# Moving the sample states' turns and updates out of the group scans and beside the feed-forward layers, with new pools for the merge

## The chip, the cores and the metric

The kernel runs on one core of a Trainium2 chip. Five engines work side by side, each in its own order: TensorE (PE; PEld is its loading of weights), VectorE (DVE), ScalarE (ACT), GpSimd (POOL) and SyncE (SP), which here only issues transfers. An instruction starts when what stands before it on its engine is done and the semaphores that it waits for have come. The metric is the time of one execution in microseconds (us), as the median of several runs. A profiled execution gives the trace from which the rows below are read.

## The reference

One layer of a hybrid decoder is applied to 512 prompt rows and to 64 sample rows (8 sequences of 8 new positions), all in fp32:

```
h  = x + 0.5 * SwiGLU_1(rms(x))
u  = rms(h) @ W_in   -> z | xBC | dt | q | k | v | f | g_ssd | g_att
y_ssd = SSD(z, conv(xBC), dt)      (4 groups of 8 heads, state 64 x 128 per head, chunks of 128)
y_att = attention(q, k, v, f)      (the samples also see 2048 cached rows each)
h  = h + W_out(sigmoid(g_ssd) * (y_ssd @ W_ssd) + sigmoid(g_att) * (y_att @ W_att))
y  = h + 0.5 * SwiGLU_2(rms(h))
```

The part that matters here is the recurrent state of the samples. Each of the 8 sequences brings a state h0 of 32 heads x 64 x 128, and its 8 rows are one short chunk of the scan:

```
y_off[t]  = exp(acs[t]) * (C[t] . h0)              the old state seen by the new rows
h_new     = exp(acs[last]) * h0 + sum_s w[s] * x[s] (outer) B[s]     the new state, an output
```

## The kernel before

The 576 rows stand as columns: an activation tile has 128 features on its partitions and 576 columns, worked in two halves of 288. Every fp32 product is made of three products of fp32r operands: value = hi + lo, and hi·hi, hi·lo and lo·hi are summed in one PSUM bank (`mm3`, lines 208 to 210). For a weight block, loaded by SP in "stage" tiles of 512 KB (four buffers), `split` makes hi on ACT (`whi`, line 173) and lo on DVE or POOL (`wlo`, line 174), four buffers each. For an activation, `hilo` does it with an ACT copy (line 217) and a DVE subtraction (line 218).

The stages follow each other: the first feed-forward layer (to about 560 us, with the start of the input projection, 22 hidden blocks in two parts of 12 and 10, each followed by 8 output blocks), input projection and attention (to about 1010 us), the scans of the four groups (1010 to 1400 us), the last group's output and the merge of the two branches, the product with W_out (to about 1460 us), and the second feed-forward layer (to the end).

In a group's scan stand the convolution of the next group (`group_in`, `xr` at line 1046), the chunks of the prompt (`chunk`, with the decay tiles `dk`, line 1216, and the diagonal product, line 1241), the state carried from chunk to chunk, the gate (`gate`, with `zt` loaded from DRAM into one buffer), and eight of the 32 sample states. A state tile is 128 x (4 x 128), 256 KB: four sequences of one pair of heads. `state` loads it (`h0`), turns it with four TensorE transposes (line 1273), copies the turned tile with ACT (`hT`, line 1275), multiplies it with C (`cz`, line 1277), multiplies the unturned tile with its decay on POOL (`decp`, line 1278), makes the update with one matmul (line 1280), adds it on DVE (line 1281) and stores the tile. The operands of the update matmul are built in the function `updates` from 96-partition tiles that SP and ACT gather. Three buffers of the tag `h0` serve the states and these gathered tiles.

The merge follows group_out of the last group. For each of eight column tiles j it loads `th` (SP) and `mt` (ACT) from DRAM, computes (th + 1)·accs on DVE (line 1358), adds mt on POOL (line 1359, the last tile on DVE), and splits the sum into `xh` and `xl`. The product with W_out needs all eight split tiles for each of its eight column blocks; `hts`, loaded from hD at line 1369, is added at line 1380.

The code is written in the order of the stages, but a scheduler of the framework decides each engine's order from a timeline that it simulates itself; `soon()` raises the priority of what stands in it. Buffers of a pool are given out again when the last reader of the former tile is done, and an instruction that writes into one waits for that.

## Time and profile before

| | before |
|---|---|
| median of 3 runs | 1915.45 us (1914.47 to 1915.89) |
| profiled execution | 1914.71 us |
| its span, first to last instruction | 1912.9 us |
| granted TensorE clock, mean | 0.988 of full speed |
| TensorE busy | 1840.0 us, 96% |
| DVE, ACT, POOL busy | 1065.6, 748.2, 652.2 us |
| moved by DMA | 243.21 MB, 127 GB/s in the mean |

Busy times are sums over the whole span, so they say which engine is nearest to its limit but not where; the views by stretch do that. In a row of groups, "x32 | 39.8, 1244 | 3.7 <-PE tr L1273 3.7" means 32 instructions, 39.8 us together, 1244 ns in the mean, and 3.7 us in which the engine stood still ahead of them, ended by TensorE's tr at line 1273. ACTq, SPq and DVEq are the engines' queues: issues of transfers and waits for semaphores, which are not counted as busy. A clock of 1.00 is full speed, 2.4 GHz; 0.50 is the lower level, 1.2 GHz.

### The profile page before, as it was taken

The numbers are of one execution on the slowest core, as the hardware profiler recorded it, in microseconds if no ns is written. First come the engines' busy times: TensorE is split into PE (matmuls) and PEld (weight loads), VectorE is DVE, ScalarE is ACT, GpSimd is POOL, SyncE is SP. The second block draws the span as 40 slices with busy tenths as digits, with TensorE's granted clock in tenths as the row PEclk, the third lists the DMA queues.
The fourth block names the chain that finished last, engine by engine and source line by source line (L and its number), as shares of the span: only waits on it lengthen the run. The fifth ranks groups of instructions, "written<-read, shape, count | busy, mean of one in ns | idle before, by whom it ended". The sixth has DMA issues, their size and how long they took to land. (4 is left out here: it accounts for less than half of the span.)

```text
span 1912.9 us, 38609 instructions
## 1 busy us (share of the span) xinstructions
PE 1840.0 (96%) x15335; PEld 1731.7 (91%) x15335; DVE 1065.6 (56%) x2204; ACT 748.2 (39%) x1553; POOL 652.2 (34%) x719
## 2 busy tenths in 40 slices
PE   7999999999998999999998988989999999999999
PEld 7999999999896888888997877878889999999998
DVE  4554334445234777775729767888785544334432
ACT  4233223334222555554427455555434333223322
POOL 0433012322322344432227455675744233003310
PEclk9999999999998999999999999999999999999999
DMA  5432223234534787865465545464654332222322
GB/s 152 112 96 80 89 78 89 83 105 111 145 109 129 188 255 223 246 200 148 95 174 153 141 127 142 111 178 124 174 155 136 89 88 77 80 74 81 88 90 71
DMA packets 270841, 243.21 MB, mean 127 GB/s; under 512 B 53276, under 2 KB 243404, under 8 KB 270508
## 3 DMA queue, kind: packets, MB, share of 16 engines
q1 hardware_dynamic: 208208, 169.35, 32.4%
q10 hardware_dynamic: 53092, 36.79, 6.4%
q0 software_dynamic: 9360, 34.61, 5.6%
q8 instruction: 121, 1.98, 0.4%
q14 instruction: 60, 0.49, 0.1%
HBM read 204.97 MB, written 29.03 MB: 122 GB/s over the span
## 5 line engine op out<-in xcount | busy, mean ns | idle before, releaser
L173 ACT ACTIVATE whi<-stage 128x512 fp32r<-128x512 f32 (+2 forms) x474 | 294.6, 622 | 732.4 <-PE acc L209 640.6
L208 PE MATMUL acc<-xh,whi 128*128 128x288 f32 x1856 | 561.7, 303 | 17.8 <-DVE xr L1046 11.5
L209 PE MATMUL acc<-xl,whi 128*128 128x288 f32 x1856 | 552.6, 298 | 0.0
L210 PE MATMUL acc<-xh,wlo 128*128 128x288 f32 x1856 | 552.3, 298 | 0.0
L174 DVE TENSOR_TENSOR wlo<-stage,whi 128x512 fp32r<-128x512 f32 (+1 forms) x373 | 271.9, 729 | 263.9 <-ACT whi L173 243.8
L208 PEld LDWEIGHTS acc<-xh,whi 128*128 128x128 f32 x1856 | 351.0, 189 | 24.8 <-DVE xr L1046 11.5
L209 PEld LDWEIGHTS acc<-xl,whi 128*128 128x128 f32 x1856 | 351.3, 189 | 2.1 <-issue 1.5
L210 PEld LDWEIGHTS acc<-xh,wlo 128*128 128x128 f32 x1856 | 350.7, 189 | 2.0 <-issue 1.3
L338 POOL TENSOR_TENSOR u<-u,s 128x288 f32<-128x288 f32 x88 | 92.1, 1048 | 484.3 <-DVE u L337 427.7
L208 PE MATMUL pv<-xh,whi 128*128 128x288 f32 (+1 forms) x784 | 231.4, 296 | 2.4 <-ACT xh L220 2.2
L209 PE MATMUL pv<-xl,whi 128*128 128x288 f32 (+1 forms) x784 | 231.9, 296 | 0.6 <-DVE xl L218 0.6
L210 PE MATMUL pv<-xh,wlo 128*128 128x288 f32 (+1 forms) x784 | 231.6, 296 | 0.0
L174 POOL TENSOR_TENSOR wlo<-stage,whi 128x512 fp32r<-128x512 f32 (+1 forms) x101 | 138.2, 1368 | 269.6 <-ACT whi L173 255.6
L208 PEld LDWEIGHTS pv<-xh,whi 128*128 128x128 f32 (+1 forms) x784 | 147.3, 188 | 2.9 <-ACT xh L220 2.4
L209 PEld LDWEIGHTS pv<-xl,whi 128*128 128x128 f32 (+1 forms) x784 | 147.2, 188 | 1.2 <-DVE xl L218 0.8
L210 PEld LDWEIGHTS pv<-xh,wlo 128*128 128x128 f32 (+1 forms) x784 | 147.2, 188 | 0.2
L340 POOL TENSOR_TENSOR hl<-u,hh 128x288 fp32r<-128x288 f32 x88 | 77.5, 882 | 81.6 <-ACT hh L339 81.6
L208 PE MATMUL pv<-hh,whi 128*128 128x288 f32 x352 | 104.4, 296 | 0.0
L209 PE MATMUL pv<-hl,whi 128*128 128x288 f32 x352 | 104.3, 296 | 0.0
L208 PE MATMUL acc<-hh,whi 128*128 128x288 f32 x352 | 104.1, 296 | 0.0
L210 PE MATMUL acc<-hh,wlo 128*128 128x288 f32 x352 | 104.1, 296 | 0.0
L209 PE MATMUL acc<-hl,whi 128*128 128x288 f32 x352 | 104.1, 296 | 0.0
(335 smaller groups left out, 3470.0 us busy)
## 6 DMA issues: line engine op xcount, KB each, us to landing
stage<-in_w_in_dram SPq DMA_DIRECT2D x52, 512.0 KB
stage<-in_ffn_w_up_dram SPq DMA_DIRECT2D x44, 512.0 KB
stage<-in_ffn_w_gate_dram SPq DMA_DIRECT2D x43, 512.0 KB
stage<-in_ffn_w_down_dram SPq DMA_DIRECT2D x40, 512.0 KB
pb<-pastD SPq DMA_DIRECT2D x32, 256.0 KB
ab<-cumD SPq DMA_DIRECT2D x32, 256.0 KB
h<-in_state_ssm_dram SPq DMA_DIRECT2D x32, 256.0 KB
out_dram<-h ACTq DMA_DIRECT2D x32, 256.0 KB
```

Of the source, the lines that this page charges most:

```text
L173: act(hi, view, AF.Copy)
L174: e.tensor_tensor(lo, view, hi.bitcast(F32), ALU.subtract)
L208: mm(out, lhsT=hi, rhs=a, start=first and i == 0, stop=False)
L209: mm(out, lhsT=hi, rhs=b, start=False, stop=False)
L210: mm(out, lhsT=lo, rhs=a, start=False, stop=last and i == n - 1)
L338: G.tensor_tensor(u, u, sil[half], ALU.mult)
L340: G.tensor_tensor(hl[:, hs(half)], u, hh[:, hs(half)].bitcast(F32), ALU.subtract)
```

## The change

A state is taken apart into three pieces. Its turning (`turns`) is done beside the first feed-forward layer: from the fifth hidden block on, behind each block, one state is loaded, transposed, copied by ACT and stored turned to DRAM (`hTD`). Its product with C stays in the scan, where `state` now loads the turned tile into one of four buffers. Its update (`updates`) is done beside the second feed-forward layer, one state behind each block: the scan only stores the update's operands to DRAM (`operands`, into `upxD` and `upbD`); there they are loaded, the state is loaded a second time, and the decay product and the addition are one fused DVE operation for each of four pieces of 128 x 128, with the matmul's PSUM bank as its second operand. `decp` moves to the pool that lives for the whole kernel. `zt` has two buffers in place of one.

The merge is written into two new pools: `mg`, with three buffers each for `th` and `mt`, and `mhl`, with eight each for the split tiles `mh` and `ml`. Before, it took its tiles from the scan's pools, and its split tiles from the pool that held the mixer's operands; that place is now taken by the operands of the last norm. In the scan's pool, small tiles that shared the tags `h0` and `hT` now share a tag `x4`.

```diff
...
+    def place(h, t):
+        return (4 * h * 32 + 2 * t) * 64 * P, [(P, P), (32 * 64 * P, 4), (1, P)]
...
+    def turns(wait):
+        for _ in range(wait):
+            yield
+        with pool("turn", side="right", reuse_waits="tile") as sp_:
+            for t in range(16):
+                for h in range(2):
+                    h0 = tl(sp_, [P, 4, P], tag="h0", bufs=4)
+                    nc.sync.dma_start(out=h0, in_=ap3(A["state_ssm"][0], *place(h, t)))
+                    ps = tr()
+                    for b in range(4):
+                        nc.tensor.transpose(ps[:, b * P:(b + 1) * P], h0[:, b, :], ident)
+                    hT = tl(sp_, [P, 512], tag="hT", bufs=3)
+                    act(hT, ps, AF.Copy)
+                    nc.scalar.dma_start(out=hTD[h, t], in_=hT)
+                    yield
...
+    def updates():
+        with pool("upd", side="right", reuse_waits="tile") as sp_:
+            for g in range(4):
+                for h in range(2):
+                    r = slice(32 * h, 32 * (h + 1))
+                    xu = tl(sp_, [96, 512], F32R, tag="xu", bufs=2)
+                    bu = tl(sp_, [96, P], tag="bu", bufs=2)
+                    for k, (u, v) in enumerate(((0, 0), (0, 1), (1, 0))):
+                        nc.sync.dma_start(out=xu[32 * k:32 * (k + 1)].bitcast(F32), in_=upxD[g, u, r])
+                        nc.sync.dma_start(out=bu[32 * k:32 * (k + 1)], in_=upbD[g, v, r])
+                    bs = tl(sp_, [96, 4, P], F32R, tag="bs", bufs=2)
+                    G.tensor_tensor(bs, bu.unsqueeze(1).to_broadcast([96, 4, P]), C("kb", 96).unsqueeze(2).to_broadcast([96, 4, P]), ALU.mult)
+                    for i in range(4):
+                        t = 4 * g + i
+                        h0 = tl(sp_, [P, 4, P], tag="h0", bufs=5)
+                        nc.sync.dma_start(out=h0, in_=ap3(A["state_ssm"][0], *place(h, t)))
+                        ps = tr()
+                        mm(ps, lhsT=xu[:, i * P:(i + 1) * P], rhs=bs.rearrange("k b n -> k (b n)"), start=True, stop=True)
+                        for b in range(4):
+                            V.scalar_tensor_tensor(h0[:, b, :], h0[:, b, :], decp[:, t, 4 * h + b:4 * h + b + 1],
+                                                   ps[:, b * P:(b + 1) * P], ALU.mult, ALU.add)
+                        nc.scalar.dma_start(out=ap3(O["ssm_s"][0], *place(h, t)), in_=h0)
+                        yield
...
-        ffn(nrm1, cg, A["ffn1_w_up"][0], A["ffn1_w_down"][0], hts, done1)
+        ffn(nrm1, cg, A["ffn1_w_up"][0], A["ffn1_w_down"][0], hts, done1, turns(4))
...
-    decp = tl(mixp, [P, 16, B], tag="decp")
+    decp = tl(constp, [P, 16, B], tag="decp")
...
-                zt = tl(xz, [P, 4, P], tag="zt", bufs=1)[:, :, :n]
+                zt = tl(xz, [P, 4, P], tag="zt", bufs=2)[:, :, :n]
...
-            def updates(x, bp):
-                xh = tl(wk, [NS, 512], F32R, tag="hT", bufs=2)
+            def operands(x, bp):
+                xh = tl(wk, [NS, 512], F32R, tag="x4", bufs=3)
                 act(xh, x, AF.Copy)
-                V.tensor_tensor(x, x, xh.bitcast(F32), ALU.subtract)
+                xl = tl(wk, [NS, 512], F32R, tag="x4", bufs=3)
+                V.tensor_tensor(xl, x, xh.bitcast(F32), ALU.subtract)
                 bh = tl(wk, [NS, P], F32R, tag="cbm", bufs=3)
                 act(bh, bp, AF.Copy)
                 bl = tl(wk, [NS, P], tag="cbm", bufs=3)
                 V.tensor_tensor(bl, bp, bh.bitcast(F32), ALU.subtract)
...
+                nc.scalar.dma_start(out=upxD[g, 0], in_=xh.bitcast(F32))
+                nc.scalar.dma_start(out=upxD[g, 1], in_=xl.bitcast(F32))
+                nc.scalar.dma_start(out=upbD[g, 0], in_=bh.bitcast(F32))
+                nc.scalar.dma_start(out=upbD[g, 1], in_=bl)
...
-            def state(h, i, ob, xs_, bs):
-                o = (4 * h * 32 + g * 8 + 2 * i) * 64 * P
-                dims = [(P, P), (32 * 64 * P, 4), (1, P)]
-                h0 = tl(wk, [P, 4, P], tag="h0", bufs=3)
-                nc.sync.dma_start(out=h0, in_=ap3(src, o, dims))
-                t = tr()
-                for b in range(4):
-                    nc.tensor.transpose(t[:, b * P:(b + 1) * P], h0[:, b, :], ident)
-                hT = tl(wk, [P, 512], tag="hT", bufs=2)
-                act(hT, t, AF.Copy)
+            def state(h, i, ob):
+                hT = tl(wk, [P, 512], tag="hT", bufs=4)
+                nc.sync.dma_start(out=hT, in_=hTD[h, 4 * g + i])
                 for b in range(4):
                     mm(ob[b * 32:(b + 1) * 32, :P], lhsT=cz[:, 4 * h + b, :], rhs=hT[:, b * P:(b + 1) * P], start=h == 0, stop=h == 1)
-                G.tensor_tensor(h0, h0, decp[:, 4 * g + i, 4 * h:4 * h + 4].unsqueeze(2).to_broadcast([P, 4, P]), ALU.mult)
-                s = tr()
-                mm(s, lhsT=xs_[:, i * P:(i + 1) * P], rhs=bs.rearrange("k b n -> k (b n)"), start=True, stop=True)
-                V.tensor_tensor(h0, h0, s.rearrange("p (b n) -> p b n", n=P), ALU.add)
-                nc.scalar.dma_start(out=ap3(dst, o, dims), in_=h0)
...
-                    state(h, c, ob, *ops[h])
+                    state(h, c, ob)
...
-        mhl = []
-        for j in range(8):
-            th = tl(xz, [P, NT], tag="cT" if j % 2 else "bT", bufs=2)
-            nc.sync.dma_start(out=th, in_=thD[:, 8 + j, :])
-            mt = tl(xz, XR, tag="xr", bufs=2)[:, :NT]
-            nc.scalar.dma_start(out=mt, in_=mattD[:, j, :])
-            V.scalar_tensor_tensor(th, th, 1.0, accs[j], ALU.add, ALU.mult)
-            (G if j < 7 else V).tensor_tensor(th, th, mt, ALU.add)
-            mhl.append(hilo(xp, th, "xh", "xl"))
     hp2 = ctx.enter_context(pool("h2", side="right", reuse_waits="tile"))
     hts = [tl(hp2, [P, NT], tag=f"h{k}") for k in range(8)]
-    x2p = ctx.enter_context(pool("x2", bufs=8, side="right", reuse_waits="tile"))
     with mixes:
-        with pool("mg", reuse_waits="tile") as mg:
+        with pool("mhl", bufs=8, side="right", reuse_waits="tile") as mp, pool("mg", side="right", reuse_waits="tile") as mg:
+            mhl = []
+            for j in range(8):
+                th = tl(mg, [P, NT], tag="th", bufs=3)
+                nc.sync.dma_start(out=th, in_=thD[:, 8 + j, :])
+                mt = tl(mg, [P, NT], tag="mt", bufs=3)
+                nc.scalar.dma_start(out=mt, in_=mattD[:, j, :])
+                V.scalar_tensor_tensor(th, th, 1.0, accs[j], ALU.add, ALU.mult)
+                (G if j < 7 else V).tensor_tensor(th, th, mt, ALU.add)
+                mhl.append(hilo(mp, th, "mh", "ml"))
             for j in range(8):
                 nc.scalar.dma_start(out=hts[j], in_=hD[:, j, :])
             wide[0] = True
             co = Cols(A["w_out"][0], 0)
-            nrm3 = Norm(16, mg, x2p)
+            nrm3 = Norm(16, mg)
...
-        ffn(nrm3, Cols(A["ffn2_w_gate"][0], 0), A["ffn2_w_up"][0], A["ffn2_w_down"][0], hts, done2)
+        ffn(nrm3, Cols(A["ffn2_w_gate"][0], 0), A["ffn2_w_up"][0], A["ffn2_w_down"][0], hts, done2, updates())
...
```

First place. On TensorE, in one chunk of the first group's scan, stood ahead (names: `mm` the chunk's products, `pv` the outputs, `tr` the transposed state and the update, `hst` the carried state):

```order
L1254 MATMUL mm_12627<-xde_12593,bt_12597 128x512
L1202 MATMUL mm_12670<-cT_11363,bT_11279 128x128
L1277 MATMUL pv_12522<-hT_12530,cz_12359 32x128 x4
L1273 MATMUL tr_12543<-ident_76,h_2295_12541 128x128 x4
L1280 MATMUL tr_12555<-bs_12447,xs_12445 128x512
L1241 MATMUL pv_12599<-dk_12566,xdt_12591 64x128
L1243 MATMUL pv_12599<-ab_12564,hst_12520 64x128
```

and stands now:

```order
L1288 MATMUL pv_12969<-ab_12945,hst_12913 64x128
L1299 MATMUL mm_12997<-xde_12963,bt_12967 128x512
L1313 MATMUL pv_13002<-hT_13003,cz_12686 32x128 x4
L1313 MATMUL pv_13002<-hT_13009,cz_12686 32x128 x4
L1247 MATMUL mm_13032<-cT_11690,bT_11606 128x128
L209 MATMUL acc_13504<-xl_5181,whi_13497 128x288
L210 MATMUL acc_13504<-xh_5180,wlo_13498 128x288
```

The four transposes of `h` and the update matmul into `tr` are gone; the product of `hT` with `cz` has stayed, and the weights' matmuls of the next group follow it.

Second place. On DVE, at the merge, stood ahead (`u` and `accs` are the last group's outputs being scaled and summed, `bT` and `cT` the merge's tiles, `xl` their low parts):

```order
L1336 TENSOR_TENSOR accs_2243_12356<-accs_2243_12356,u_17808 128x288
L1358 SCALAR_TENSOR_TENSOR cT_17935<-cT_17935,accs_2243_12356 128x576
L218 TENSOR_TENSOR xl_17932<-bT_17925,xh_17931 128x576
L1334 TENSOR_TENSOR u_17830<-acc_17817,ssq_16683 128x288
L1336 TENSOR_TENSOR accs_2244_12357<-accs_2244_12357,u_17830 128x288
L1334 TENSOR_TENSOR u_17846<-acc_17833,ssq_16683 128x288
L1336 TENSOR_TENSOR accs_2244_12357<-accs_2244_12357,u_17846 128x288
L174 TENSOR_TENSOR wlo_18063<-stage_17992,whi_18062 128x512
L1358 SCALAR_TENSOR_TENSOR bT_17945<-bT_17945,accs_2244_12357 128x576
L218 TENSOR_TENSOR xl_17942<-cT_17935,xh_17941 128x576
```

and stands now (`th` and `ml` are the merge's tiles and their low parts):

```order
L174 TENSOR_TENSOR wlo_17930<-stage_17859,whi_17929 128x512
L1365 TENSOR_TENSOR u_17733<-acc_17720,ssq_16665 128x288
L1367 TENSOR_TENSOR accs_2344_12685<-accs_2344_12685,u_17733 128x288
L1365 TENSOR_TENSOR u_17749<-acc_17736,ssq_16665 128x288
L1367 TENSOR_TENSOR accs_2344_12685<-accs_2344_12685,u_17749 128x288
L1393 SCALAR_TENSOR_TENSOR th_17771<-th_17771,accs_2337_12678 128x576
L1393 SCALAR_TENSOR_TENSOR th_17781<-th_17781,accs_2338_12679 128x576
L218 TENSOR_TENSOR ml_17778<-th_17771,mh_17777 128x576
L1393 SCALAR_TENSOR_TENSOR th_17791<-th_17791,accs_2339_12680 128x576
L218 TENSOR_TENSOR ml_17788<-th_17781,mh_17787 128x576
```

The products with `accs` (then line 1358, now 1393) stood between the last group's sums; now all eight stand behind the last of them, and a low part follows only when its product is through POOL and ACT.

On ACT, at the same place, stood ahead (`xr` is the merge's second operand, `whi` the high part of a weight block):

```order
L1357 DMA xr_17937<-mattD_84 128x576
L173 ACTIVATE whi_18000<-stage_17994 128x512
L217 ACTIVATE xh_17931<-bT_17925 128x576
L1357 DMA xr_17947<-mattD_84 128x576
L173 ACTIVATE whi_18062<-stage_17992 128x512
L217 ACTIVATE xh_17941<-cT_17935 128x576
L1357 DMA xr_17957<-mattD_84 128x576
L173 ACTIVATE whi_18066<-stage_17994 128x512
```

and stands now (`mt` is the merge's second operand; `whi_17929` and `whi_17933` belong to the second column block of W_out, and the buffer that `whi_17933` takes is the one that the last matmul of the last group's output frees):

```order
L173 ACTIVATE whi_17867<-stage_17861 128x512
L173 ACTIVATE whi_17929<-stage_17859 128x512
L173 ACTIVATE whi_17933<-stage_17861 128x512
L1392 DMA mt_17773<-mattD_84 128x576
L1392 DMA mt_17783<-mattD_84 128x576
L1392 DMA mt_17793<-mattD_84 128x576
L217 ACTIVATE mh_17777<-th_17771 128x576
L1392 DMA mt_17803<-mattD_84 128x576
L217 ACTIVATE mh_17787<-th_17781 128x576
L1392 DMA mt_17813<-mattD_84 128x576
```

The loads of `mattD` stood one by one between copies and splits; now the first three stand together behind `whi_17933`, and each later one behind a copy into `mh`.

Third place. On SP, in the first feed-forward layer, stood ahead (stage tiles of weights only):

```order
L161 DMA stage_1385<-in_ffn_w_up_dram 128x4x256
L161 DMA stage_1387<-in_ffn_w_up_dram 128x4x256
L161 DMA stage_1599<-in_ffn_w_gate_dram 128x4x256
L161 DMA stage_1601<-in_ffn_w_gate_dram 128x4x256
L161 DMA stage_1673<-in_ffn_w_up_dram 128x4x256
L161 DMA stage_1675<-in_ffn_w_up_dram 128x4x256
```

and stands now:

```order
L161 DMA stage_1411<-in_ffn_w_up_dram 128x4x256
L161 DMA stage_1413<-in_ffn_w_up_dram 128x4x256
L373 DMA h_223_1175<-in_state_ssm_dram 128x4x128
L373 DMA h_248_1325<-in_state_ssm_dram 128x4x128
L373 DMA h_277_1483<-in_state_ssm_dram 128x4x128
L373 DMA h_302_1633<-in_state_ssm_dram 128x4x128
L373 DMA h_331_1791<-in_state_ssm_dram 128x4x128
L373 DMA h_356_1941<-in_state_ssm_dram 128x4x128
L161 DMA stage_1645<-in_ffn_w_gate_dram 128x4x256
L161 DMA stage_1647<-in_ffn_w_gate_dram 128x4x256
```

Six loads of states stand ahead of the next pair of stage tiles; their tiles have four buffers.

## Rows read from the trace of the kernel before

**Rows 1.** The profile's page: busy time of each engine, and GB/s in 40 slices.
```profile
PE 1840.0 (96%) x15335; PEld 1731.7 (91%) x15335; DVE 1065.6 (56%) x2204; ACT 748.2 (39%) x1553; POOL 652.2 (34%) x719
...
GB/s 152 112 96 80 89 78 89 83 105 111 145 109 129 188 255 223 246 200 148 95 174 153 141 127 142 111 178 124 174 155 136 89 88 77 80 74 81 88 90 71
```
**Rows 2.** Busy time by stretch: start:end, us, PE, PEld, DVE, ACT, POOL, clock, DMA, GB/s.
```profile
70.00:560.00 490.00, 489.34 (x3636) 478.63 (x3635) 198.74 (x370) 149.59 (x270) 122.61 (x131) 1.00 0.36 98
1010.00:1400.00 390.00, 356.61 (x2869) 315.40 (x2868) 309.15 (x574) 209.30 (x481) 242.79 (x249) 0.98 0.52 145
1400.00:1442.00 42.00, 38.50 (x281) 37.23 (x280) 38.05 (x56) 12.67 (x20) 18.47 (x12) 1.00 0.52 150
1490.00:1880.00 390.00, 390.00 (x2948) 390.00 (x2947) 158.59 (x300) 115.50 (x215) 85.34 (x88) 1.00 0.29 87
```
**Rows 3.** TensorE's waits, 1010 to 1400 us: who waited for whom, total, times, longest.
```profile
PE acc L208 <- DVE xr L1046: 10.3, 4, 3.5
PE pv L1241 <- DVE dk L1216: 6.8, 2, 5.0
PE tr L1280 <- DVE h L1281: 2.5, 3, 1.2
PE pv L1277 <- ACT hT L1275: 2.4, 3, 1.3
...
PE tr L1273 <- DVE h L1281: 2.0, 2, 1.2
```
**Rows 4.** TensorE's timeline around one state: start, us, line, operation, tiles, count.
```profile
1362.46 0.40 PE L1280 MATMUL tr<-bs,xs 96*128 96x512 f32 x1
1362.70 0.30 PE L210 MATMUL acc<-xh,wlo 128*128 128x288 f32 x1
...
1365.51 0.66 PE L1273 MATMUL tr<-ident,h 128*128 128x128 f32 x4
1366.01 0.27 PE L1225 MATMUL mm<-ident,xg 128*128 128x128 f32 x1
```
**Rows 5.** Groups by line and shape: count, busy us, mean ns, idle before.
```profile
L1278 POOL TENSOR_TENSOR h<-h,decp 128x512 f32<-128x512 f32 x32 | 39.8, 1244 | 3.7 <-PE tr L1273 3.7
...
L1281 DVE TENSOR_TENSOR h<-h,tr 128x512 f32<-128x512 f32 x32 | 21.7, 680 | 12.3 <-POOL h L1278 12.3
...
L1245 DVE SCALAR_TENSOR_TENSOR xg<-xg,dsk,pv 128x128 f32<-128x128 f32 x64 | 17.9, 339 | 1.4 <-PE pv L1243 1.2
```
**Rows 6.** Line 1281 in DVE's queue: ns as min/median/max, first and last start.
```profile
L1281 DVEq EVENT_SEMAPHORE  x37: 21/50/3150, 1023.5 to 1378.6; - x37
```
**Rows 7.** The chain that ended last, 1048 to 1062 us: start, us, what.
```profile
1050.10 7.01 DMA zt<-zD
```
**Rows 8.** Line 491, the page history's stores, issued by ACT: ns as min/median/max.
```profile
L491 ACTq DMA_DIRECT2D pastD<-lg x32: 310/463/1685, 81.3 to 99.4; - x32
```
**Rows 9.** Timelines of the first layer: TensorE at 103.8 us, SP's queue at 115 us.
```profile
103.79 0.29 PE L208 MATMUL acc<-xh,whi 128*128 128x288 f32 x1
...
115.05 1.33 SPq L161 DMA_DIRECT2D stage<-in_ffn_w_gate_dram  x2
```
**Rows 10.** Groups of ACT, POOL and DVE at the merge, 1395 to 1450 us.
```profile
L173 ACT ACTIVATE whi<-stage 128x512 fp32r<-128x512 f32 x16 | 10.0, 630 | 26.0 <-PE acc L209 24.1 <-DMA h<-hD 1.9
L217 ACT ACTIVATE xh<-bT 128x576 fp32r<-128x576 f32 x4 | 2.7, 687 | 4.6 <-POOL bT L1359 4.6
...
L1359 POOL TENSOR_TENSOR bT<-bT,xr 128x576 f32<-128x576 f32 x4 | 6.6, 1658 | 13.4 <-DVE bT L1358 13.4
...
L218 DVE TENSOR_TENSOR xl<-cT,xh 128x576 fp32r<-128x576 f32 x4 | 3.0, 752 | 0.2 <-ACT xh L217 0.2
```
**Rows 11.** Line 1369, loads from hD, in ACT's queue: ns as min/median/max, first and last.
```profile
L1369 ACTq DMA_DIRECT2D h<-hD x8: 326/345/443, 1439.5 to 1442.9; - x8
```
**Rows 12.** DVE's timeline at the first addition behind w_out.
```profile
1442.48 0.46 DVE L1380 SCALAR_TENSOR_TENSOR h<-pv,h 128x288 f32<-128x288 f32 x1 [1.53 <-PE acc L209]
```
**Rows 13.** Busy time where attention starts, columns as in rows 2.
```profile
598.00:620.00 22.00, 16.01 (x66) 10.83 (x64) 8.83 (x20) 7.14 (x16) 6.14 (x14) 0.61 0.55 154
```

More of the change, by code (lines that the diff above doesn't have):

```diff
@@ L349, in ffn @@
                             V.scalar_tensor_tensor(hv, a, 0.5, hv, ALU.mult, ALU.add)
+                    next(beside, None)
                     if hi_f == NF:
                         done(j)
+            for _ in beside:
+                pass
+    def place(h, t):
[15 more added lines that the diff above has]
+                    yield
```

31 lines of the change are left out of this document (10 added, 21 removed).

## Prediction

> **What bounds the kernel now.** I read the busy times first: TensorE is busy 1840.0 of 1912.9 us, DVE 1065.6, ACT 748.2, POOL 652.2 [rows 1]. TensorE is the bound, so an edit can gain only where TensorE waits, or where its work goes away. The second view, busy time by stretch, says where that is [rows 2]: in the two feed-forward layers TensorE is never idle (489.3 of 490 us; 390.0 of 390), in the four group scans it is idle 390 − 356.6 = 33.4 us at a mean clock of 0.98, and at the last group's output 42 − 38.5 = 3.5 us. The third, TensorE's waits in the scans, names what ends them [rows 3]: DVE above all (xr 10.3 us, dk 6.8 us, of which one is 5.0), then the sample states themselves: the update waits 2.5 us for h, the product with C 2.4 us for hT, a turn 2.0 us for h's buffer (in a row of its own, the last of this group). DVE is busy 309 of these 390 us, POOL 243.
>
> **Moved TensorE work.** Each of 32 states has four transposes (0.50 us from the first to the matmul behind them) and one update matmul (0.24 us, the next starting 1362.70 − 1362.46) [rows 4]. So 32 × 0.50 = 16.0 us go from the scans to layer 1, and 32 × 0.24 = 7.7 us to layer 2. Both layers are full, so each grows by that, and if the scans were as full they would shrink by the same 23.7 us. I set this at 0: what counts is the waiting.
>
> **What the scans get back.** The chain of a state goes: load, transposes, ACT copy, POOL product with the decay (1244 ns, 32 of them), update matmul, DVE add (680 ns), store. Out of the scans go POOL's 39.8 us, DVE's 21.7 us and the 12.3 us in which DVE stood still for POOL's h [rows 5]. Since DVE runs in order, such a wait holds all behind it: one lasted 3.15 us [rows 6], and I put the 5.0 us wait for dk down to it. Direct: 2.5 + 2.4 + 2.0 + 5.0 = 11.9 us. Of the other 33.4 − 11.9 = 21.5 us a third, 7 us, because DVE gives 34 us less to states and POOL's chain loses its wait for the one zt buffer (7.0 us, [rows 7]). At a mean clock of 0.98 some 390 × 0.02 = 8 us are lost to the lower level; with fewer waits half of it, 4 us, comes back. Against it stand new waits for hT's transfers (four buffers, a load per state as before): 3 us. The sum is 11.9 + 7 + 4 − 3 = 20 us, bounds 0 (DVE stays full and hT is late) and 33.4 + 8 = 41 us (no wait left, full clock).
>
> In layer 2 the DVE add becomes four fused operations of a 128x128 piece, priced at 339 ns by a like one with PSUM as source [rows 5]: 32 × 4 × 0.339 = 43 us on a DVE that is busy 158.6 of 390 us [rows 2]. That hides under TensorE; without that cover, at the most the part that delays an accumulator would show, and four banks stand ready. bs is now built by POOL in layer 2 (85 of 390 us busy), hT copied by ACT in layer 1 (149.6 of 490): nothing.
>
> **The first state.** SP's first state load (the order's third place) must wait until the page history, in whose memory it lies, is stored. The last of 32 stores is issued by ACT at 99.4 us [rows 8]; with the longest time that a 288 KB load can have needed below (2.7 us) for store and load each, the state lands at 99.9 + 2.7 + 0.4 + 2.7 = 105.7 us. TensorE wants it where the matmul at 103.79 us stands [rows 9]. So it waits 1.9 us, say 2, from 0 to 6. SP's next weights stand behind six state loads (the order's third place); the sixth of these needs the second one's buffer, free after its transposes, which stand 24 matmuls behind the first state's: at 105.7 + 0.5 + 24 × 0.132 + 0.5, about 110 us. Before, the weights were loaded at 115.05 us [rows 9]: no loss.
>
> **The merge.** Here the change adds a wait. Before, the eight merge products (th × accs, plus mt, split into two) stood between the last group's outputs, and their loads were issued long ahead. Now (the order's second place) all eight stand on DVE behind the last add into accs, and on ACT the three first loads of mt stand behind the split whi_17933, whose buffer comes free with the last matmul of the group's output. Behind that matmul TensorE has nothing but the product with w_out, which starts with mh of tile 0. With L for a load from issue to landing: split 0.63, issue 0.35, L, POOL's add 1.66, ACT's copy 0.69 [rows 10], the issue from [rows 11]: the first operand comes 3.3 + L us after the last matmul. th and mt have three buffers, so tiles 3 to 5 are loaded when tiles 0 to 2 have been split: DVE's ml 0.75, L, DVE's product of the same size, taken at 0.75 too, POOL 1.66, ACT 0.69, together 3.9 + L; tiles 6 and 7 once more; tile 7 0.8 behind 6, and its 12 matmuls 1.6. Sum 3.3 + L + 2 (3.9 + L) + 2.4 = 13.5 + 3L. The 96 matmuls of the first two column blocks that fill this take 96 × 390 / 2948 = 12.7 us [rows 2]. TensorE thus stands idle 1 + 3L, in place of the 3.5 us that it lost here before.
>
> The trace does not show L alone. Lower end: eight loads of 288 KB from hD were issued from 1439.5 us on, at 0.33 us the shortest issue, and DVE used the first at 1442.48: at most 2.7 us from issue to landing [rows 11, 12]. Upper end: the 7.0 us of zt [rows 7]. I take 4, since the row of the same size is the nearer one but six loads and weights run here at once. Net: 1 + 12 − 3.5 = 9.5 us; from 5.6 (L 2.7) to 18.5 (7.0).
>
> After waits the clock falls: where attention starts with pauses it is 0.61 over 22 us [rows 13], that is 17 us at 1.2 GHz; in the scans, with 33 us of waits, it stays at 0.98 over 390 us [rows 2]. While TensorE waits that costs nothing; I take 2 us, from 0 to 8.
> The Trainium skill (TensorE: Matmul & The Clock Gate, HAM oscillation — how this bites in real kernels) says that short bursts of matmuls, each behind a transfer, stay at the lower level burst after burst. By that rule the 96 matmuls would take 25 us in place of 12.7, a round would be bound by them, and the clock would cost 7 us instead of 2: 1914 us, no change. The start of attention agrees, the scans do not: most of their waits are followed by the full clock.
>
> **Sum**, against the profiled execution (1914.71 us, 1.8 us around the span, 0.7 us under the median of 1915.45): −20 + 2 + 9.5 + 2 = −6.5, so 1908.2 us on the profiled execution and 1909 us on the median.
>
> **Rivals.**
> 1. Slower: the merge's transfers share their engines. A round loads six tiles of 288 KB, 1.77 MB; at 255 GB/s, the fastest slice of the page [rows 1], that is 6.9 us. Then L = 6.9, the merge costs 18.2 net, the clock 4 since the pauses are longer, and with 15 us from the scans: −15 + 2 + 18.2 + 4 = +9.2, 1924 us. With 20 us from the scans and 2 us of clock the time is that of before at L = 6.2, the point from which it decides. For it speaks zt's 7.0 us, against it the 2.7 us of hD, where eight loads were issued together.
> The Trainium skill (DMA: Bandwidth & Descriptors, Issuing engines are not separate DMA queues) has it that loads of SP and ACT interleave on the same 16 engines, so th on one queue and mt on the other win only issue time. No run here shows that yet.
> 2. The change does not do what it says: DVE stays the limit in the scans (its conv tiles are untouched, and they are behind the xr waits), only the direct 11.9 us come back, and the merge eats them: −12 + 14 = +2, 1917 us.
> 3. The scans become full: 36 us back, 1914.7 − 36 + 14 = 1893 us. For it speaks that DVE and POOL both lose more of their load than TensorE; against it, that DVE was full in stretches without states too.
>
> **How the numbers follow.** Forecast 0.50 (its own range 1900 to 1915), rival 1 0.22, rival 2 0.15, rival 3 0.13. A measurement here can tell 0.2% (3.8 us) from no change. Faster than 1911.6: four fifths of the forecast and rival 3, 0.53. Slower than 1919.3: rival 1 and a little of rival 2, 0.25. The rest 0.22. The range 1895 to 1924 leaves out the outer part of rivals 1 and 3.
>
> **What would show it.** After the change: both feed-forward layers longer by 16 and 8 us with TensorE full; the wait for h and the DVE queue's 3 us stop gone from the scans, their idle time near 15 us; a wait of about 7 us in front of the first matmul with mh, then two more of 2 to 4 us, the last of them some 24 us behind the last group's output. The forecast is wrong if the merge costs over 15 us, if the scans' idle time stays near 33 us, or if TensorE waits in layer 1 or 2 for a state.

## The result, and the profile after

The changed kernel takes 1905.0 us (1901.77 to 1907.87, four runs) against 1914.96 us of before: a ratio of 0.9945, 95% interval 0.9930 to 0.9961. Forecast were 1909 us, 1895 to 1924. Its profiled execution spans 1903.9 us, 9.0 less than before.

The page's first rows of the changed kernel, which answer to [rows 1]: TensorE has the same work, POOL 47 us less, and TensorE's share of the span has risen.

```profile
PE 1840.5 (97%) x15335; PEld 1736.0 (91%) x15335; DVE 1061.4 (56%) x2300; ACT 745.0 (39%) x1545; POOL 604.9 (32%) x687
```

Busy time by stretch, columns as in [rows 2], of the changed kernel: the feed-forward layers are as full as before but for the first state's wait in layer 1, the scans wait 17.2 us in place of 33.4, and the 42 us that were the last group's output before now hold the merge's waits, at a clock of 0.84.

```profile
70.00:580.00 510.00, 506.79 (x3775) 495.68 (x3775) 197.88 (x372) 167.49 (x303) 122.76 (x131) 1.00 0.44 127
1010.00:1400.00 390.00, 372.78 (x3031) 336.19 (x3029) 302.28 (x608) 205.70 (x482) 208.71 (x219) 0.99 0.47 138
1400.00:1442.00 42.00, 33.18 (x203) 31.07 (x204) 29.23 (x32) 14.76 (x24) 20.18 (x13) 0.84 0.47 141
1490.00:1880.00 390.00, 390.00 (x2926) 388.62 (x2925) 180.63 (x396) 112.89 (x209) 78.36 (x90) 1.00 0.43 124
```

TensorE's waits over the whole span, columns as in [rows 3]: those for the states' h in the scans are gone, the 10.3 us for xr in the scans are 3.0 in all, and two new ones stand here, for the merge's first operand (8.5 us at once) and for the first state (2.4 us).

```profile
PE pv L208 <- ACT mh L217: 10.2, 4, 8.5
...
PE acc L208 <- DVE xr L1101: 3.0, 2, 1.8
PE tr L376 <- DMA h<-in_state_ssm_dram: 2.4, 1, 2.4
...
PE pv L209 <- DVE ml L218: 1.5, 1, 1.5
...
PE pv L1286 <- DVE dk L1261: 0.6, 2, 0.4
```

To see where the 9.0 us come from, I cut both spans at TensorE's instructions that both kernels have: the last matmul with a hidden operand of layer 1, the first and the last diagonal product of the scans (pv from dk and xdt), the last norm's statistics, and the last matmul with a hidden operand of layer 2. Times between them in us, read from TensorE's timelines:

```
                                        before    after    change   forecast
up to layer 1's last hidden operand     449.96   468.27    +18.3    +16.0 turns, +2 first state
to the first diagonal product           555.94   554.56     -1.4      0
to the last diagonal product            370.64   323.90    -46.7    -43.7 (20 and the moved 23.7)
to the last norm's statistics           112.16   125.51    +13.3    +11.5 (9.5 and 2 of clock)
to layer 2's last hidden operand        418.60   425.99     +7.4     +7.7
```

These are pieces of one execution each. In the runs with the same code in layer 1, its piece took 465.2 to 468.3 us, so a piece is not good to better than some 3 us.

Next the merge in the changed kernel. ACT's timeline shows the three loads of mt behind the split that the last matmul releases, and the first copy into mh 7.13 us later:

```profile
1397.07 0.63 ACT L173 ACTIVATE whi<-stage 128x512 fp32r<-128x512 f32 x1 [2.62 <-PE acc L209]
1397.10 1.29 ACTq L1392 DMA_DIRECT2D mt<-mattD  x3
1404.83 0.68 ACT L217 ACTIVATE mh<-th 128x576 fp32r<-128x576 f32 x1 [7.13 <-POOL th L1394]
```

POOL's timeline has the sum that it waits for. It starts behind mt's landing, which the trace has at 1403.27; the row names DVE, whose second product ended at the same time:

```profile
1403.40 1.39 POOL L1394 TENSOR_TENSOR th<-th,mt 128x576 f32<-128x576 f32 x1 [4.19 <-DVE th L1393]
```

From 1397.43, the end of the first issue (1397.10 and 0.33), to the landing are 5.8 us. The six loads of the first round took 3.3 to 7.0 us from issue to landing by the trace, the ten later ones 2.5 to 4.0. In the first round the transfers are near their limit (a DMA share of 0.95 in the last column but one, at 339 GB/s). The third column from the end is the clock:

```profile
1400.00:1405.00 5.00, 0.00 (x0) 0.00 (x0) 1.30 (x2) 0.17 (x1) 1.59 (x2) 0.63 0.95 339
1405.00:1410.00 5.00, 4.43 (x17) 4.15 (x18) 2.57 (x3) 1.78 (x3) 3.03 (x2) 0.50 0.77 209
1415.00:1420.00 5.00, 3.66 (x24) 2.96 (x22) 4.87 (x4) 2.41 (x4) 4.25 (x3) 1.00 0.75 208
```

### The profile page after: what moved, and what is told of

Its sections match the earlier page's. It is cut to its first block, busy times and chain, and to the rows that moved or that the text cites. A ratio compares the mean times of both kernels' runs of the same rounds, so it can differ in the third digit from the quotient of the medians.

```text
span 1903.9 us, 38768 instructions
## 1 busy us (share of the span) xinstructions
PE 1840.5 (97%) x15335; PEld 1736.0 (91%) x15335; DVE 1061.4 (56%) x2300; ACT 745.0 (39%) x1545; POOL 604.9 (32%) x687
## 3 DMA queue, kind: packets, MB, share of 16 engines
q8 instruction: 121, 1.98, 0.4%
## 4 chain that ended last, share of the span: by engine, by line
PE 84%; DVE 5%; DMA 4%; ACT 3%; issue 1%; POOL 1%; ACTq 1%; POOLq 0%; DVEq 0%; SPq 0%
PE acc L208 16%; PE acc L209 16%; PE acc L210 16%; PE pv L209 7%; PE pv L208 7%; PE pv L210 7%; PE tr L907 2%; PE tr L897 1%; PE mm L834 1%; PE pv L865 1%; PE mm L852 1%; PE pv L1286 1%; PE pv L945 1%; PE tr L376 1%; PE tr L934 1%
## 5 line engine op out<-in xcount | busy, mean ns | idle before, releaser
L208 PE MATMUL acc<-xh,whi 128*128 128x288 f32 x1792 | 543.3, 303 | 9.2 <-ACT tt L1116 4.2
L209 PE MATMUL acc<-xl,whi 128*128 128x288 f32 x1792 | 534.6, 298 | 0.0
L210 PE MATMUL acc<-xh,wlo 128*128 128x288 f32 x1792 | 533.7, 298 | 0.0
L209 PEld LDWEIGHTS acc<-xl,whi 128*128 128x128 f32 x1792 | 340.1, 190 | 1.6 <-issue 1.2
L208 PE MATMUL pv<-xh,whi 128*128 128x288 f32 (+1 forms) x720 | 214.5, 298 | 2.0 <-ACT xh L220 2.0
L209 PE MATMUL pv<-xl,whi 128*128 128x288 f32 (+1 forms) x720 | 213.2, 296 | 0.0
L210 PE MATMUL pv<-xh,wlo 128*128 128x288 f32 (+1 forms) x720 | 212.8, 296 | 0.1
L208 PEld LDWEIGHTS pv<-xh,whi 128*128 128x128 f32 (+1 forms) x720 | 135.5, 188 | 2.5 <-ACT xh L220 2.3
L209 PEld LDWEIGHTS pv<-xl,whi 128*128 128x128 f32 (+1 forms) x720 | 135.3, 188 | 1.2
L210 PEld LDWEIGHTS pv<-xh,wlo 128*128 128x128 f32 (+1 forms) x720 | 135.2, 188 | 0.5 <-DVE wlo L174 0.3
```

What stands on the lines that cost most here:

```text
L208: mm(out, lhsT=hi, rhs=a, start=first and i == 0, stop=False)
L209: mm(out, lhsT=hi, rhs=b, start=False, stop=False)
L210: mm(out, lhsT=lo, rhs=a, start=False, stop=last and i == n - 1)
```

## The experiments

Each was timed in five rounds against the kernel before on the same chip; the ratio is to that kernel, so the changed kernel's 0.9945 is what they are compared with. "Scans" is the stretch from the first diagonal product to the last group's last output matmul, with TensorE's busy time in it.

**The merge.** First the old merge in the changed kernel; the tiles of `updates` move into the mixer's operand place so that all fits.

```diff
-                th = tl(mg, [P, NT], tag="th", bufs=3)
+            th = tl(xz, [P, NT], tag="cT" if j % 2 else "bT", bufs=2)
...
-                mhl.append(hilo(mp, th, "mh", "ml"))
+            mhl.append(hilo(xp, th, "xh", "xl"))
...
-            nrm3 = Norm(16, mg)
+            nrm3 = Norm(16, mg, x2p)
...
-                        h0 = tl(sp_, [P, 4, P], tag="h0", bufs=5)
+                        h0 = tl(xp, [P, NT], F32R, tag="xh").bitcast(F32)[:, :512].rearrange("p (b n) -> p b n", n=P)
```

> The changed kernel with the merge as it was before (its tiles in the scan's pools, its split tiles in the mixer's operand place, the last norm's operands in a pool of their own); the updates beside layer 2 take their tiles from the mixer's operand place instead. Theory (the merge is a cost of its own): in the changed kernel the stretch from the last group's output to the last norm's statistics is 75.4 us long, 20.2 more than before, of which 2.0 are 15 matmuls that only changed sides, 11.7 are waits and 6.5 the lower clock; with the old merge about 18 us go, less some 3 us of waits before the last output that come back: 1888 to 1891 us. Rival (the merge has to wait for the sums in either form, since the scans now end 53 us earlier with the same transfers): not over 6 us of it come back, 1899 us or more.

Measured: 0.9869 (0.9846 to 0.9891), 14.5 us faster than the changed kernel. The piece behind the last output is 55.28 us again, exactly that of before, and the piece ahead of it 6.96 us longer. The expectation had 3 us for that last part; the new merge had taken more work out of there (15 matmuls, 2.0 us, and the old merge's DVE products between the sums). The new merge thus costs 20.15 − 6.96 = 13.2 us net; between the kernel before and the changed one it was 13.3 in the table above.

Then the opposite, the new merge in the kernel before, states untouched:

```diff
-            mhl.append(hilo(xp, th, "xh", "xl"))
...
+                mhl.append(hilo(mp, th, "mh", "ml"))
...
-            nrm3 = Norm(16, mg, x2p)
+            nrm3 = Norm(16, mg)
```

> The kernel before with the new merge alone: new pools for the merge, the last norm's operands in the mixer's place, states untouched. Theory (waits behind whi_17933 and on the transfers, and then the lower clock): 12 us of waits and 6 us of clock are added, 2 to 3.5 us of waits ahead of the last output are saved: 1929 to 1932 us, with the granted clock near 0.85 over the 42 us behind the last output. Rival (the new merge is slow only because the shorter scans leave its transfers no time): under 1921 us.

Measured: 1.0066 (1.0042 to 1.0091), 12.7 us slower. The piece behind the last output is 75.91 us, as in the changed kernel (75.43), though the scans are as slow as before. So the merge's cost is its own. The expected 14 to 17 us were too many, again by what it saves ahead of the output.

Then the lower clock: 64 transposes fill the first wait.

```diff
             nrm3 = Norm(16, mg)
+            scr = sm()
+            for k in range(64):
+                nc.tensor.transpose(scr[:, (k % 4) * P:(k % 4 + 1) * P], accs[7][:, NT - P:], ident)
```

> The changed kernel with 64 transposes of a tile of the last group's sums, whose result nobody reads, ahead of the product with W_out: they fill TensorE's 8.5 us wait for the first merge operand (some 8 us of work at full clock) and have nothing else to do. Theory (the lower clock behind the wait costs 6.5 us, and comes from the wait): the granted clock from 1400 to 1442 us rises from 0.84 to over 0.95 and the time falls by 4 to 6 us, to 1899 to 1901 us. Rival (the first matmuls wait for their operands anyway, so their lower clock is hidden by the waits that follow): the clock rises, the waits behind grow by as much, 1904 to 1906 us.

Measured: 0.9938 (0.9914 to 0.9962), no difference. The clock came back:

```profile
1400.00:1442.00 42.00, 36.50 (x260) 34.37 (x259) 26.55 (x32) 13.97 (x22) 19.66 (x13) 0.96 0.48 151
```

but from the last output to the last norm's statistics TensorE needed 74.78 us in place of 75.43. The waits behind the first became longer, as its waits from 1395 to 1430 us show (3.2 and 2.3 us, against 1.7 and 1.5 of the changed kernel behind its first wait of 8.5):

```profile
PE pv L208 <- ACT mh L217: 3.2, 3, 2.1
PE pv L209 <- DVE ml L218: 2.3, 3, 1.2
```

So the operands set the pace, and the lower clock cost some 0.7 us, as far as the transposes took it away (0.96 is not yet 1.00). My own reading in the first expectation, 11.7 us of waits and 6.5 of clock, fell. The Trainium skill (TensorE: Matmul & The Clock Gate, HAM oscillation — how this bites in real kernels) tells of bursts behind transfers that run at the lower level, each one again. The 0.50 behind the wait of 8.5 us agrees. Behind the later waits, none of them over 1.5 us, the clock was 1.00 from 1415 to 1420 us, so the 7 us that the prediction worked out from that rule did not come.

Last, eight buffers in place of three, so that no load waits for a buffer.

```diff
-                th = tl(mg, [P, NT], tag="th", bufs=3)
+                with soon():
+                    th = tl(mg, [P, NT], tag="th", bufs=8)
...
```

> The changed kernel with eight buffers each for th and mt in place of three, the loads at raised priority: all 16 loads of 288 KB are issued together behind whi_17933 and the stage tile, and the two later rounds of waiting for a buffer are gone. Theory (the transfers share the bandwidth: 4.7 MB at the 339 GB/s that the changed kernel moved from 1400 to 1405 us take 14 us, so the last tile is there 15 to 16 us after the last output in place of 22, and product, sum and split follow): 5 to 7 us faster than the changed kernel. Rival (a load takes its 2.7 us however many run, and POOL's 1.66 us per tile sets the pace): 10 to 13 us faster, the whole cost of the merge but for the first wait.

Measured: 0.9927 (0.9911 to 0.9943), 3.4 us by the medians' ratio; the intervals of the two overlap. TensorE finished the first two column blocks 28.6 us behind the last output, before 30.9. So the shared bandwidth is nearer than a fixed time for a load, but both expectations were too high. The 16 loads were not in flight at once either. ACT's eight issues stretch over 9.74 us, since a new load starts only when an earlier transfer has landed and given back its semaphore, of which the trace has eight (ACT's fourth load starts at 1399.61, 0.02 us behind the landing of a stage tile):

```profile
1397.70 9.74 ACTq L1393 DMA_DIRECT2D mt<-mattD  x8
```

With up to eight loads in flight the transfers stood at their limit and the first wait grew to 10.6 us:

```profile
1400.00:1405.00 5.00, 0.00 (x0) 0.00 (x0) 2.27 (x3) 0.00 (x0) 0.60 (x1) 0.56 0.97 334
1405.00:1410.00 5.00, 1.39 (x5) 1.05 (x5) 2.86 (x3) 1.94 (x3) 5.00 (x4) 0.50 1.03 379
```

The last load landed 15.7 us behind the last output by the trace, as the theory had it. The two column blocks ended 12.9 us later still: what is left there is the work of DVE, POOL and ACT on the tiles. The loads of SP and ACT stood at one common limit, which agrees with the Trainium skill (DMA: Bandwidth & Descriptors, Issuing engines are not separate DMA queues), by which they run on the same 16 DMA engines; no run here issued all of them from one queue.

**The first state.**

```diff
-        ffn(nrm1, ..., done1, turns(4))
+        ffn(nrm1, ..., done1, turns(6))
```

> The changed kernel with the turning of the states begun two hidden blocks later (behind the seventh). Theory: the one wait in layer 1, 2.35 us for the first state, is gone and nothing takes its place: 1902.5 us. Rival (the store of the page history is not what the first load waits for, or SP's weights come later in its place): the wait stays or moves, 1905 us.

Measured: 0.9924 (0.9901 to 0.9947); between 80 and 470 us the wait for the state is gone, and one of 0.9 us for wlo stands there. The intervals overlap, so only the profile shows it.

**Which move pays.** One half of the change each, both with the old merge:

```diff
 turn_only (on the kernel before)
+        ffn(nrm1, ..., done1, turns(4))
-                transposes of h0 into t; act(hT, t, AF.Copy)
+                nc.sync.dma_start(out=hT, in_=hTD[h, 4 * g + i])
 update_only (on merge_old)
-        ffn(nrm1, ..., done1, turns(4))
+        ffn(nrm1, ..., done1, iter(()))
-                nc.sync.dma_start(out=hT, in_=hTD[h, 4 * g + i])
+                load of h0, its transposes into t; act(hT, t, AF.Copy)
```

> The kernel before with the turning alone moved beside layer 1: the scan loads the turned tile besides the unturned one, decay product, update matmul, addition and merge stay as before. Theory (what came back in the scans is the update's chain over POOL and DVE, which stays here): only the waits for hT and for a turn, 2.4 and 2.0 us, can go, and 2 us come in for the first state: 1 to 4 us faster than before. Rival (the scans are short of TensorE, and any work that leaves them returns more than it costs in layer 1): 8 to 12 us faster.

> The changed kernel with the old merge (updates beside layer 2, tiles in the mixer's place), but the states are turned in the scan as before, and zt has one buffer. Theory (the update's chain is what the scans waited for): 15 to 20 us faster than before, two thirds or more of the 25 us that the kernel with both moves and the old merge gained. Rival (half and half): 8 to 13 us faster.

Measured: turn_only 1.0014 (0.9999 to 1.0029), update_only 0.9829 (0.9810 to 0.9847), both together with the old merge 0.9869. The update alone (with the old merge and one zt buffer) gives 33 us, more than any expectation, and the turning gives nothing alone and takes some 8 us where the update has gone. The scans of the kernel before, of merge_old, of turn_only and of update_only, in this order:

```profile
1005.90:1433.40 427.50, 389.96 (x3114) 346.86 (x3115) 343.84 (x626) 223.43 (x508) 260.46 (x260) 0.98 0.52 145
```
```profile
1023.50:1403.10 379.60, 363.31 (x2955) 326.56 (x2955) 307.66 (x594) 203.73 (x467) 214.34 (x220) 0.99 0.48 138
```
```profile
1021.80:1433.50 411.70, 379.64 (x2987) 335.63 (x2987) 335.66 (x626) 207.41 (x476) 254.13 (x260) 0.98 0.59 171
```
```profile
1004.00:1392.40 388.40, 376.47 (x3079) 338.79 (x3078) 303.12 (x593) 216.76 (x496) 213.96 (x220) 1.00 0.47 135
```

TensorE stands still for 37.5, 16.3, 32.1 and 11.9 us in them, the first number less the second. With the update gone, the turning back in the scans costs 388.4 − 379.6 = 8.8 us there; in layer 1 it costs 467.2 − 448.4 = 18.8 us, its first wait of 2.5 included. With the update still there it saved 427.5 − 411.7 = 15.8 us of the scans and cost 15.7 us in layer 1, a wait of 1.5 included.

**zt.**

```diff
-                zt = tl(xz, [P, 4, P], tag="zt", bufs=2)[:, :, :n]
+                zt = tl(xz, [P, 4, P], tag="zt", bufs=1)[:, :, :n]
```

> The changed kernel with one buffer for zt in place of two. Theory (POOL's wait of 7.0 us for zt held the group's end, and the second buffer takes it away): the waits in the scans grow by 2 to 4 us and the time by as much. Rival (the state's chain hid behind it, the second buffer is worth nothing here): within 1 us of the changed kernel.

Measured: 0.9954 (0.9937 to 0.9971), the scans 373.4 against 374.0 us. The theory fell: the 7.0 us of [rows 7] lay on the chain that ended last, but with the state's work gone one buffer is enough.

**What the scans were short of.** Into the changed kernel's `state`, behind the load of hT, one piece at a time, its result unread:

```diff
+                scr = tl(wk, [P, 512], tag="scr", bufs=1)
 pool_back, chain_back
+                G.tensor_tensor(scr, hT, decp[...], ALU.mult)
 chain_back
+                V.tensor_tensor(scr, scr, hT, ALU.add)
 dve_back
+                V.tensor_tensor(scr, hT, hT, ALU.add)
 dve_free
+                V.tensor_tensor(scr, bT[:, :512], cT[:, :512], ALU.add)
```

> The changed kernel with one POOL product of 128x512 per state put back into the scans (hT times the decay, into a tile that nobody reads): 32 x 1.24 = 40 us of POOL work, without the chain to the update and to DVE. Theory (the chain was the cost, not POOL's load: POOL is busy 209 of 390 us there): 0 to 4 us slower than the changed kernel. Rival (POOL's load holds gate and conv products that others wait for): 8 us slower or more, most of the scans' gain gone.

> The changed kernel with one DVE addition of 128x512 per state put back into the scans (hT + hT, into a tile that nobody reads): 32 additions of 0.7 to 1.4 us, 22 to 45 us of DVE work, without a wait for POOL. Theory (the cost was DVE standing still for POOL's product, in order, with dk, xdt and the sums queued behind it): 0 to 5 us slower than the changed kernel. Rival (DVE is at its limit in the scans, so its load alone was the cost): 10 us slower or more.

> The changed kernel with the pair put back: POOL's product of hT with the decay and behind it DVE's addition on the same tile, so that DVE waits for POOL again; nobody reads the result. Theory (the stall is a cost of its own): over 4 us more than the product alone (8 us over the changed kernel by the medians) and the addition alone together. Rival (the two loads simply add up): the sum of the two within 3 us.

> The changed kernel with one DVE addition of 128x512 per state put back into the scans, now of two operands that lie ready from before the group's scan (B and C, into a tile that nobody reads), so that DVE waits for nothing. With hT as operand DVE worked 34.1 us more and stood still 14.6 us for hT's transfers, and the scans grew by 20.5 us. Theory (DVE's load is the limit): 15 us slower than the changed kernel or more. Rival (those 14.6 us of standing still, with work queued behind, were the cost): under 8 us slower.

The groups of the added instructions, first of dve_back, then of chain_back, then of dve_free, show how long they took and what DVE stood still for:

```profile
L1313 DVE TENSOR_TENSOR scr<-hT 128x512 f32<-128x512 f32 x32 | 34.1, 1067 | 14.6 <-DMA hT<-hTD 14.6
```
```profile
L1313 POOL TENSOR_TENSOR scr<-hT,decp 128x512 f32<-128x512 f32 x32 | 37.9, 1183 | 21.1 <-DMA hT<-hTD 12.1 <-DVE scr L1314 9.0
L1314 DVE TENSOR_TENSOR scr<-scr,hT 128x512 f32<-128x512 f32 x32 | 33.4, 1044 | 4.3 <-POOL scr L1313 4.3
```
```profile
L1313 DVE TENSOR_TENSOR scr<-bT,cT 128x512 f32<-128x512 f32 x32 | 26.0, 813 | 0.1
```

Not all of the 32 lie in the stretch of the scans as it is cut here. Within it are, of dve_free and of dve_back:

```profile
L1313 DVE TENSOR_TENSOR scr<-bT,cT 128x512 f32<-128x512 f32 x26 | 20.9, 806 | 0.0
L1313 DVE TENSOR_TENSOR scr<-hT 128x512 f32<-128x512 f32 x30 | 32.8, 1092 | 14.2 <-DMA hT<-hTD 14.2
```

| | added to DVE, and stood still | scans (changed kernel 374.0) | ratio |
|---|---|---|---|
| pool_back | none (POOL 39.5 us) | 378.0 | 1.0000 (0.9988 to 1.0012) |
| dve_back | 34.1 and 14.6 | 394.5 | 1.0077 (1.0062 to 1.0091) |
| chain_back | 33.4 and 4.3 (POOL 37.9) | 397.4 | 1.0070 (1.0051 to 1.0090) |
| dve_free | 26.0 and 0.1 | 386.9 | 1.0025 (1.0010 to 1.0040) |

POOL's load alone costs 4.0 us of the scans by the profile, 10 us by the ratio (the intervals leave 5 at the least). The profiled execution was the fastest of twelve, so the times speak for the rival of pool_back and the profile for its theory; the size stays open. DVE's load costs much: 20.9 us that wait for nothing lengthen the scans by 12.9 us, and the 26.0 in all lengthen the time by some 15 us. In dve_back 32.8 us with 14.2 of standing still lengthen the scans by 20.5 us. That is 0.62 and 0.63 us per us of work, so the standing still shows no cost of its own. And chain_back, which has the wait for POOL back, is no slower than dve_back: some 24 us over the changed kernel, where product and addition alone came to 10 and 25. So the theory that the stall behind POOL was a cost of its own fell, its rival, that the two loads add up, was too high as well, and DVE's load holds. These runs do not separate it from what DVE's additions do to POOL beside them (busy 211.1 us in dve_free's scans, 205.4 in the changed kernel's).

## Why the prediction was right

**Time and range.** 1905.0 against 1909, within the forecast's own range, and the moves of layers 1 and 2 came as worked out: 32 turns 15.9 us (forecast 16.0), 32 update matmuls 7.4 (7.7), the first state 2.4 (2): it was to land at 105.7 us, and the first turn of the changed kernel starts at 106.6, by the view of that line (ns as min/median/max, first and last start):

```profile
L376 PE MATMUL tr<-ident,h x128: 269/272/303, 106.6 to 452.4; 128*128 128x128 f32 x128
```

The spread of these pieces is larger than such agreement, so part of it is luck: the same wait for the first state took 1.5 to 3.3 us in the other runs that have it. The four fused additions of a state hid wholly, at the price that the like row gave:

```profile
L403 DVE SCALAR_TENSOR_TENSOR h<-h,decp,tr 128x128 f32<-128x128 f32 x128 | 35.7, 341 | 0.0
```

**The merge's mechanism was right, its terms were mis-sized.** TensorE's first matmul with mh started 8.5 us behind the end of the last output, where 3.3 + L gives 7.3 at the L = 4 that was taken. The load itself took 5.8 us, but the split's 0.63 us did not stand ahead of it: the issue began 0.03 us after the split. The first two column blocks ended at 30.9 us, where 13.5 + 3L gives 25.5. Of these 5.4 us more, 1.2 fall on the first operand, 2.3 on the two later rounds, and 1.9 on the last tile and the matmuls behind it. In the later rounds the loads took 2.5 to 4.0 us, so there L = 4 was not too small. What took longer were the products (ns as min/median/max): DVE's a median of 1293 ns where 0.75 us was taken, POOL's 1805 where 1.66 us was:

```profile
L1393 DVE SCALAR_TENSOR_TENSOR th<-th,accs x8: 744/1293/1978, 1399.8 to 1421.6; 128x576 f32<-128x576 f32 x8
L1394 POOL TENSOR_TENSOR th<-th,mt x7: 1394/1805/2038, 1403.4 to 1421.1; 128x576 f32<-128x576 f32 x7
```

In all, 9.5 us and 2 of clock were forecast, and 13.3 measured, with some 0.7 of clock in it. The lower end taken for L, 2.7 us from hD's loads, held for the first of those eight only: by the same trace the eighth took 5.3 us from issue to landing, so what many loads do to L stood in the trace of before. The transfers that share their engines (rival 1) came true in the first round. What kept the kernel ahead was that the scans gave 23.4 us, not rival 1's 15.

**The scans: the size right, the reasons half wrong.** Forecast 20 us beyond the moved work, measured 46.7 − 15.9 − 7.4 = 23.4. That the two are near is in part luck. With the old merge and the turns left where they were, moving the update alone shortened the scans by 39.1 us, 31 more than its own TensorE work, and moving the turns as well shortened them by 8.8 us more, where 16 of work had left. The prediction saw neither. Three steps behind the 20 do not hold:
- "I set this at 0", for the moved TensorE work. For the update's 7.7 us it may stand; for the turns it fails. They cost 15.7 to 18.8 us in layer 1, where TensorE is never idle, and return 15.8 us while DVE holds the scans and 8.8 us once it does not. Part of their time in the scans had stood in TensorE's waits: with the update gone it stands still 11.9 us with the turns there, 16.3 without.
- "Direct: 2.5 + 2.4 + 2.0 + 5.0": the waits for h, hT and dk went, but to take them away did not take the waiting away. In turn_only, with hT from DRAM, TensorE still stands still 32.1 us in the scans. Its waits for dk are shorter than before, with the update still there, and those for xdt, another DVE product, are the longest:

```profile
PE pv L1269 <- DVE xdt L1256: 10.5, 5, 4.2
PE pv L1269 <- DVE dk L1244: 2.1, 3, 1.2
```

  So these waits name whichever DVE result is late. Why it is late shows where the 5.0 us for dk stand, which end at 1129.46 us. The prediction put them down to DVE's stop of 3.15 us for POOL's h [rows 6]; that one stands at 1378.6 us, 249 us later. Ahead of them one split of a weight tile, wlo, held DVE for 7.61 us, while POOL ran eight instructions without a pause between them, of which these are the first and the last:

```profile
1119.91 7.61 DVE L174 TENSOR_TENSOR wlo<-stage,whi 128x512 fp32r<-128x512 f32 x1
1119.86 1.30 POOL L1219 TENSOR_TENSOR ab<-ab,cT 128x512 f32<-128x512 f32 x1
1126.52 0.45 POOL L1159 TENSOR_TENSOR ssq<-sq 128x128 f32<-128x128 f32 x1
```

  One of the eight was a state's decay product. A second such stop took 5.8 us, and turn_only has two, of 4.9 and 5.4. Where the update is gone no DVE instruction of the scans took over 2.1 us.
- zt's share of the 7 us: nothing.

What held is the remaining reason, that DVE is busy for less time. In the scans of update_only DVE is busy 303.1 us in place of 343.8. Not only the additions went: with POOL's products away, most of DVE's other products of two SBUF operands became shorter, and dk longer. In the scans of the kernel before, then of the changed kernel:

```profile
L174 DVE TENSOR_TENSOR wlo<-stage,whi 128x512 fp32r<-128x512 f32 x41 | 44.2, 1079 | 14.7 <-ACT whi L173 14.6
L1216 DVE TENSOR_TENSOR dk<-dk,cbm 128x512 f32<-128x512 f32 x32 | 30.8, 968 | 10.2 <-ACT dk L1215 9.6
```
```profile
L174 DVE TENSOR_TENSOR wlo<-stage,whi 128x512 fp32r<-128x512 f32 x41 | 30.5, 743 | 17.4 <-ACT whi L173 17.3
L1261 DVE TENSOR_TENSOR dk<-dk,cbm 128x512 f32<-128x512 f32 x32 | 39.1, 1241 | 4.4 <-ACT dk L1260 4.0
```

With POOL's product put back wlo has 890 ns. The means differ by how many instructions had one of POOL beside them (over 60 ns of overlap, counted in the traces). Alone, wlo and dk took 680 to 687 ns in the mean in both kernels; beside POOL, wlo took 1454 ahead and 797 after, dk 1065 and 1321. A DVE product with an operand in PSUM, xdt, took 677 to 683 either way. The merge shows it one by one: the four of DVE's eight products that ran with no POOL instruction beside them took 0.74 to 0.76 us, the other four 1.83 to 1.98. Two of them, and the POOL sum beside the second:

```profile
1410.82 0.75 DVE L1393 SCALAR_TENSOR_TENSOR th<-th,accs 128x576 f32<-128x576 f32 x1
1411.83 1.91 DVE L1393 SCALAR_TENSOR_TENSOR th<-th,accs 128x576 f32<-128x576 f32 x1 [0.26 <-DMA th<-thD]
1411.70 1.43 POOL L1394 TENSOR_TENSOR th<-th,mt 128x576 f32<-128x576 f32 x1 [2.31 <-DVE th L1393]
```

The Trainium skill (SBUF — State Buffer, SBUF: two separate sides) has DVE and POOL share a port that one of them holds for a whole instruction, DVE with two SBUF operands among those; these rows agree.

How much of the scans' gain DVE explains is an estimate, not shown. At the 0.62 us per us of dve_free the 40.7 us are worth 25 us, and with the update matmul's 7.7 that is 33 of the 39.1 us that update_only's scans lost. If dve_free's 12.9 us are put down to the 14.6 us by which DVE's busy time rose in its scans (310.1 against 295.6), it is 36 and 44. POOL's 4.0 us are not added, since with its product put back DVE was busier too (304.3 us). No added work brought back stops of DVE such as the 7.6 us, so these runs price DVE's load and not the stops. The loads and buffers that the update took out of the scans with it were not tried apart.

Of the rivals, the third did not come: the scans are not full, with TensorE idle 13.6 of 374.0 us in the changed kernel and 11.9 of 388.4 in update_only. The time of that rival is beaten all the same by the best version run, update_only, at 0.9829: updates beside layer 2, turns where they were, the old merge.

## What to carry to other kernels

Work that leaves a stretch for a full engine elsewhere pays its whole time there; it returns that much only if the stretch was short of that same engine. Find by adding a piece of unread work to one engine which one a stretch is short of: the names in the list of waits tell whose result was late, not why. And a move that frees memory or gives it to another stage is a change of its own, here worth 13 us against; time it apart. When several loads are issued together, price the last of them, not the first.

## What was not expected of the hardware

A clock that falls to 0.50 behind a wait cost about 0.7 us, since the operands of the matmuls came no faster. Loads of 288 KB on two queues, up to eight in flight, moved 334 to 379 GB/s at a DMA share of 0.97 to 1.03 over slices of 5 us; the fastest slice of the page before [rows 1], of 48 us, had 255. Of eight such loads issued one behind the other by ACT in the kernel before, the first took 2.6 us from issue to landing and the eighth 5.3. The added DVE additions of 128x512 took 679 to 681 ns in the mean with no POOL instruction beside them, with hT as operand and with operands that lay ready alike; beside one, 1270 (21 of 32) in dve_back, 1128 (26) in chain_back and 932 (17) in dve_free. So POOL made the difference between their means of 1067, 1044 and 813. And one DVE instruction stood 7.6 us behind eight of POOL's, to 0.55 us after the end of the last.
